# Decode steps emitted ahead of the first MLP, and the later attention's first q and k loaded amid the decode

## The chip, the cores and the metric

The kernel runs on one core of one Trainium2 chip. The metric is the device time of one launch in microseconds. Five engines work side by side, each through its own list of instructions in a fixed order: TensorE (matmuls and transposes, PE in the profile), VectorE (DVE), ScalarE (ACT), GpSimd (POOL) and SyncE (SP, which here mainly issues DMAs). An instruction that waits holds up all that stand behind it on its engine. The time before is 1550.24 us, the median of 3 runs (1548.09 to 1552.9).

## The reference

One layer of a hybrid decoder is computed for a prompt of 1024 tokens (width 1024) and for 32 sample tokens: 8 sequences of 4 tokens, each with 1024 earlier tokens whose K and V lie in a cache of 128-token pages, found through a page table.

```python
h = rms_norm(x, n1) * (1 + sc1) + sh1
proj = h @ w_in                       # 3 x 512 for attention, 4 x 512 for HGRN2
q_a, k_a = rms_norm(q_a, qg), rms_norm(k_a, kg)          # 8 heads x 64
z = einsum(q, k) * SB_SCALE + bias                       # stick-breaking attention
log_1m = where(valid, log_sigmoid(-z), 0)                # valid: key before query
w = where(valid, exp(log_sigmoid(z) + tail(log_1m)), 0)  # tail: sum over the later keys
o_a = einsum(w, v)
o_b = HGRN2(q, f, i, g, state)                           # gated recurrence, new state out
x = x + g1 * (concat(o_a, o_b) @ w_out)
h2 = rms_norm(x, n2) * (1 + sc2) + sh2
x = x + g2 * (square(relu(h2 @ w_up)) @ w_down)          # up to 4096, down to 1024
```

For the sample tokens K and V of the attention are the pages of the cache followed by the new tokens (the "decode"). Outputs are the two x, the new k and v, and the HGRN2 states.

## The kernel before

Weights and activations are split into a high and a low part, and each product is three matmuls (high x high, low x high, high x low; lines 204 to 206 and 1228 to 1230). The order of the work is: projections to about 200 us; HGRN2 and the attention of prompt tokens 0 to 511 to about 500; the output projection of these tokens, four token tiles of 128 (t = 0 to 3), to about 560; then a long stretch to about 1105 in which the first MLP (tokens 0 to 511) is interleaved with the decode and with the "later" attention (tokens 512 to 1023 against all 1024 keys); then the second output projection and the last MLP.

The output projection of a token tile ends in the residual `xr`, whose norm is worked out by ScalarE (`jk`, line 1167) and VectorE (lines 1169 to 1172); TensorE then transposes it (`ptx`, line 318), ScalarE scales it to `hf` (line 323) and VectorE splits it into `h_hi` and `h_lo` (lines 335, 336), the input of the MLP.

The first MLP goes through the hidden width in blocks of four pieces m = 0 to 3 of 128 columns. In its first block the up products are done for tokens 0 to 255 first (`pm`, 24 matmuls of 128x256 for each m), as these are ready before the tokens of tile 3, and then for tokens 256 to 511. The PSUM banks are given out by name: `M0 = "0123"` gives the four m of the first half the banks 0 to 3, `BM` gives later MLP tiles banks 0 and 1, and `BD = dict(z="4572", t="63", a="7")` gives the decode's transposes `ptd` banks 4, 5, 7 and 2 in turn, and its scores `pzd` banks 6 and 3. Whoever is emitted first gets a bank first.

The decode (line 563) builds its constants and the tile `qbd`, then walks through 64 K pages: a page is loaded by SP into `raw` (line 616, `NRAW = 4` buffers), transposed by TensorE (`ptd`, line 632, four transposes), copied to `kt` by ScalarE or VectorE (line 633), and after four pages their scores are added to `pzd` (line 638). `pzd` is copied to `dbe` (line 640) after 16 pages. Then two rounds `gz` (heads' halves of the batch) build `qbf` (line 645), the sigmoid weights `dbe` and `dom` (lines 653 to 660), and the V pages follow, interleaved with the decode of HGRN2. The attention (line 879) loads, for every head, `qh`, `ql` and `kk` from the scratch `qkd` and `vhl` from `vd`, all issued by POOL (lines 891 to 894, two buffers each), and computes scores `pz` (lines 905, 906).

Two generators, the MLP and `decode_and_attention`, are emitted in turn by `interleave`, with weights 64 and 166. A scheduler puts the instructions on each engine's list by their priority, which follows the order of emission, and by when it expects them to be ready; the lists are fixed when the program is built.

```python
interleave((mlp(*h2, [slice(0, 512)], rp, 2, ga), WM), (decode_and_attention(), W[3]))
```

Of the kernel before, what the change touches and what calls it, by code (L numbers as in the profile page):

```python
# [9 lines left out]
F32 = mybir.dt.float32  # L10
F32R = mybir.dt.float32r
# [9 lines left out]
P = 128  # L21
D = 1024
KT = 8
T = 1024
# [8 lines left out]
W = [66, 24, 9, 166, 4]  # L33
NBE0, NBE, NHB, NWA, NU, NRW, NX2, NF = 4,8,3,4,4,4,3,3
# [25 lines left out]
WM = 64  # L60
NPR = 2
NFX = 5
NSW = 5
NPL = 2
PQ0 = 100
AG = ()
BQ = "0167"
# [14 lines left out]
def hymba_step(ctx, tc, x_p, x_s, ck, cv, st_in, ptab, c_p, c_s, w_ada, b_ada, n1g, n2g, w_in,  # L82
# [3 lines left out]
    V, S, G, TE = nc.vector, nc.scalar, nc.gpsimd, nc.tensor  # L86
# [14 lines left out]
    def pool(name, side="left", stack=ctx, **kw):  # L101
        return stack.enter_context(tc.tile_pool(name=name, bufs=1, side=side, reuse_waits="tile", **kw))
# [7 lines left out]
    qkd = dp.tile([2, 2, 4, P, T], F32, name="qkd")  # L110
# [65 lines left out]
    def interleave(*steps, last=None):  # L176

        steps = [[g, n, 0] for g, n in steps]
        while steps:
            x = min(steps, key=lambda x: (x[2] + 0.5) / x[1])  # L180
            if next(x[0], x) is x:
                steps.remove(x)
                if x[0] is last:
                    return
            x[2] += 1
# [51 lines left out]
    def bank(kind, shape, name):  # L237
        turn[kind] = turn.get(kind, -1) + 1
        tag = banks[kind][turn[kind] % len(banks[kind])]
        return psum.tile(shape, F32, name=name, tag=f"bank{tag}", bufs=1)  # L240
# [262 lines left out]
    def qkv(px):  # L503
        for what, c0 in enumerate((QA, KA, VA)):
# [22 lines left out]
            for g in range(4):  # L527
                rows = slice(256 * g, 256 * (g + 1))
                x2 = pq.tile([P, 2, 512], F32, name="x2", bufs=NX2)
                for u in range(2):  # L530
# [7 lines left out]
                    yield  # L538
                with tc.high_priority(offset=PQ if what else PQ0):
                    if what < 2:  # L540
# [19 lines left out]
                                nc.sync.dma_start(qkd[what, part, 2 * p2:2 * p2 + 2, :, rows].rearrange("a p t -> p a t"),  # L560
                                                  tt.rearrange("p a u t -> p a (u t)").bitcast(F32))

    def decode(pd_):

        qbd = pd_.tile([P, 2, 544], F32, name="qbd", tag="qbd", bufs=1)
        G.memset(qbd, 0.0)
# [38 lines left out]
        ms = pd_.tile([P, 4, NB, 4], F32, name="ms")  # L605
# [35 lines left out]
        for gz in range(2):  # L641
            be = bes[gz]

            qbf = pd_.tile([P, 4, 32], F32, name="qbf")
            G.memset(qbf, 0.0)
            for p in range(4):
                for hh in range(2):
                    rr, o = slice(64 * hh, 64 * hh + 64), 4 * hh
                    S.copy(qbf[rr, p, :].rearrange("p (b x) -> p b x", x=8)[:, :, o:o + 4],
                           qTn[rr, p, 16 * gz:16 * gz + 16].rearrange("p (b t) -> p b t", t=4))  # L650
            pz = bank("t", [P, NS], "pzn")
            for p in range(4):
                TE.matmul(pz[32 * p:32 * p + 32], qbf[:, p, :], kTn[:, p, :], start=True, stop=True)
            V.tensor_tensor(be[:, T:], pz, tb[:, gz].rearrange("p b t -> p (b t)"), op=add)
            om = pd_.tile([P, NKEY + 1], F32, name="dom", tag="dom", bufs=1)
            G.memset(om[:, NKEY:NKEY + 1], 1.0)
            S.activation(om[:, 0:NKEY], be, AF.Sigmoid, bias=rbn, scale=-1.0)
            S.activation(be, be, AF.Sigmoid, bias=rbp)
            V.tensor_tensor_scan(om[:, 0:NKEY][:, ::-1], om[:, 0:NKEY][:, ::-1], om[:, 0:NKEY][:, ::-1], 1.0, op0=mult, op1=ALU.bypass)
            V.tensor_tensor(be, be, om[:, 1:NKEY + 1], op=mult)  # L660
            yield

            wt = pd_.tile([P, 9, 4, 32], F32, name="wt", tag="qbd", bufs=1)
            for k0 in (0, 4, 8):
                n, r = (4, P) if k0 < 8 else (1, NS)
                pt = bank("z", [P, 4, P], "ptdw")
                for u in range(n):
                    TE.transpose(pt[:r, u, :], be[:, (k0 + u) * P:(k0 + u) * P + r], ident)
                for u in range(n):
                    V.tensor_copy(wt[:r, k0 + u].rearrange("p b (q y) -> p b q y", y=8), pt[:r, u, :].rearrange("p (q b y) -> p b q y", q=4, y=8))  # L670
            yield

            pn = bank("z", [P, 512], "podn")
            TE.matmul(pn, wt[:NS, 8].rearrange("p b y -> p (b y)"), vn, start=True, stop=True)
            for b4 in range(4):
                b = 4 * gz + b4
                po = bank("a", [P, 512], "pod")
                for u in range(8):
                    if u % 4 == 0:
                        vt = pd_.tile([P, 4, 512], F32, name="vt", tag="kt", bufs=NKV)  # L680
                    load_page(vt[:, u % 4, :], cv, 8 * b + u)
                    g = slice(32 * (u % 4), 32 * (u % 4) + 32)
                    TE.matmul(po[g], wt[:, u, b4, :], vt[:, u % 4, :], start=(u < 4), stop=(u >= 4))
                    if u % 4 == 3:
                        yield
                od = pd_.tile([P, 512], F32, name="od", bufs=1)
                S.copy(od, po)
                g = slice(32 * b4, 32 * b4 + 32)
                V.tensor_tensor(od[g], od[g], pn[g], op=add)
                pt = bank("t", [P, 4 * P], "ptod")  # L690
                for p in range(4):
                    TE.transpose(pt[:, p * P:(p + 1) * P], od[:, p * P:(p + 1) * P], ident)
                ot = pd_.tile([P, 544], F32, name="ot", bufs=1)
                S.copy(ot[:, 0:512], pt)
                for hh in range(2):
                    r = slice(64 * hh, 64 * hh + 64)
                    src = ot[r].rearrange("p (q x) -> p q x", x=136)[:, :, 0:128].rearrange("p q (g x) -> p q x g", g=4)
                    V.tensor_reduce(ms[r, :, b, :], src[:, :, 4 * hh:4 * hh + 4, :], axis=AX.X, op=add)
                yield
# [176 lines left out]
        with tc.high_priority(offset=PH):  # L876
            norm()

    def attention(pb, ms, nbe):

        q0, nq, nk = 256 * ms[0], 256 * len(ms), 256 * (ms[-1] + 1)
        both = lambda t, part, p, r, cs: qkd[t, part, p, r, cs].unsqueeze(0).to_broadcast([2, 64, cs.stop - cs.start])
        for p in range(4):
            for hh in range(2):
                h = 2 * p + hh
                hr = slice(64 * hh, 64 * hh + 64)

                qh, ql = (pb.tile([P, nq], F32R, name=name, bufs=2) for name in ("qh", "ql"))
                kk_ = pb.tile([P, nk], F32R, name="kk", bufs=2)
                for part, tile_ in enumerate((qh, ql)):  # L890
                    G.dma_start(tile_, both(0, part, p, hr, slice(q0, q0 + nq)))
                G.dma_start(kk_, qkd[1, :, p, hr, 0:nk])
                vhl = pb.tile([P, nk // P, P], F32R, name="vhl", bufs=2)
                G.dma_start(vhl, vd[0:nk, P * h:P * (h + 1)].rearrange("(t p) x -> p t x", p=P))
                for m in ms:
                    ws = []
                    for i in (2 * m, 2 * m + 1):
                        n = (i + 1) * P
# [26 lines left out]
                    for kb in range(0, 2 * m + 2, 2):  # L925
# [12 lines left out]
                        for a in range(2):  # L938
                            cs = slice(P, 256) if diag and a == 1 else slice(0, 256)
# [22 lines left out]
    def hgrn_decode(p1):  # L962
# [63 lines left out]
        for j in range(4):  # L1026
# [8 lines left out]
    gq, ga = qkv(pool("qkv_w", stack=xstack)), pool("ada", side="right", stack=qstack)  # L1035
    ga = ada(AP0, lambda p=ga: p.tile([P, 512], F32, name="ar", tag="ar", bufs=2),
             lambda n, p=ga: p.tile([P, 2048], F32, name="wada", bufs=NAR)[:, 0:512 * n], "ada")
# [145 lines left out]
    def mlp(h_hi, h_lo, chunks, fp, nx, side=iter(())):  # L1183
# [1 line left out]
        r_hi = [h_hi[:, k] for k in range(KT)]  # L1185
        r_lo = [h_lo[:, k] for k in range(KT)]
        n = chunks[-1].stop
        g2b = fp.tile([P, D], F32, name="g2b")
        acc = [lp.tile([P, HW], F32, name=f"acc{c}", tag="acc", bufs=8) for c in range(KT)]
        for blk in range(NBLK):  # L1190
            u_hi, u_lo, ws = [], [], []
# [20 lines left out]
            if blk == 0:  # L1212
                for cs in parts:
                    for m in range(NK):
                        up(m, cs)
                    yield
            if blk == NBLK - 1:
                nc.sync.dma_start(g2b, g2d.to_broadcast([P, D]))
            for half_ in range(2):

# [29 lines left out]
    def last_mlp(h_hi, h_lo, fp):  # L1250
# [123 lines left out]
        for blk in range(NBLK):  # L1374
            u_hi, u_lo = ([lp.tile([P, HW], F32R, name=f"u{x}{m}", tag="u", bufs=8) for m in range(NK)] for x in "hl")
            if blk >= NPL:
                up([unit_weights(blk * FB_ + 2 * P * i) for i in range(2)], u_hi, u_lo)
# [61 lines left out]
    def decode_and_attention():  # L1439
        banks.update(BD)  # L1440
        with ExitStack() as es:
            gd = decode(pool("decode", stack=es))
            for _ in range(33):
                next(gd)
                yield
            banks.update(BV)
            yield from side_by_side((gd, 28), (hgrn_decode(pool("hgrn_s", stack=es)), W[4]))
        banks.update(BA)
        with ExitStack() as es:
            yield from attention(pool("attn1", stack=es), (2, 3), NBE)  # L1450

    def h2_tiles():
        return hp2.tile([P, KT, HW], F32R, name="h2_hi", tag="h2_hi", bufs=1), hp2.tile([P, KT, HW], F32R, name="h2_lo", tag="h2_lo", bufs=1)
# [3 lines left out]
    h2 = h2_tiles()  # L1457
# [7 lines left out]
    rp = pool("res", side="right", stack=rstack)  # L1465
# [1 line left out]
    banks.update(m0=M0)  # L1467
    gate = lambda: rp.tile([P, 512], F32, name="ar", tag="xres", bufs=2)
    ga = ada(AP1, gate, lambda n: wp.tile([P, 512 * n], F32, name="wada", tag="wraw", bufs=NWR), "m")
    interleave((mlp(*h2, [slice(0, 512)], rp, 2, ga), WM), (decode_and_attention(), W[3]))  # L1470
    h2 = h2_tiles()
    banks.update(o="45", r="36", s=BS)
    with ExitStack() as es:
# [37 lines left out]
```

## Time and profile before

| | |
|---|---|
| median of 3 runs | 1550.24 us (1548.09 to 1552.9) |
| profiled execution | 1546.85 us |
| its span in the trace | 1545.1 us |
| granted TensorE clock, mean | 0.988 of full speed |
| TensorE busy | 1489.3 us (96%), 9521 matmuls and transposes |
| VectorE busy | 1083.4 us (70%) |
| ScalarE busy | 642.7 us (42%) |
| POOL busy | 345.4 us (22%) |

A wait in the trace is the idle time of an engine just ahead of an instruction, with what released it ("<-"). The time of a matmul row is longer than the distance to the next one, since matmuls overlap in the array; what one costs is the distance between starts. The granted clock is the share of its full speed at which TensorE ran; 0.50 is the lower of its two levels, 1.2 instead of 2.4 GHz.

### The profile page before, as it was taken

Reading aid. Unit: us, or ns where it says so; the run is one execution under the profiler, and the core shown is the slowest. Engines: PE = TensorE matmul, PEld = TensorE weight load, DVE = VectorE, ACT = ScalarE, POOL = GpSimd, SP = SyncE. Lnnn points to the kernel's source line nnn. Section 1 sums busy time; section 2 is a strip of 40 time slices with the busy share of each in tenths; the row PEclk is TensorE's granted clock in tenths of the full one; section 3 lists DMA queues with packets and bytes.
Section 4 is the critical chain, followed back from the end, with each engine's and each line's share of the span. In section 5 each row is a group of like instructions: output and inputs, shape, how many; then the busy total and the mean of one; then the engine's idle time right before and its main releaser. Section 6 shows DMA issues by size and latency. Waiting matters only on the chain. (4 is left out here: it accounts for less than half of the span.)

```text
span 1545.1 us, 26232 instructions
## 1 busy us (share of the span) xinstructions
PE 1489.3 (96%) x9521; PEld 1257.0 (81%) x9521; DVE 1083.4 (70%) x2288; ACT 642.7 (42%) x1219; POOL 345.4 (22%) x560
## 2 busy tenths in 40 slices
PE   7999999999999989999997999999999999999998
PEld 3666689999999787775665788888578999999998
DVE  4976438888876783455554888888688567777775
ACT  3742234443422454333232666664245533343340
POOL 0200125634210030000121676694200000000000
PEclk8999999999999999999998999999999999999999
DMA  9389873423123456668677366552654333323222
GB/s 325 118 278 309 265 231 68 106 58 92 37 77 114 140 172 219 218 216 256 199 160 121 88 133 121 119 113 74 237 164 125 105 96 96 92 84 99 84 82 86
DMA packets 249414, 223.14 MB, mean 144 GB/s; under 512 B 60507, under 2 KB 196259, under 8 KB 247236
## 3 DMA queue, kind: packets, MB, share of 16 engines
q1 hardware_dynamic: 186308, 199.26, 41.0%
q0 software_dynamic: 62976, 22.20, 8.8%
q8 instruction: 75, 1.23, 0.3%
q14 instruction: 55, 0.45, 0.1%
HBM read 190.14 MB, written 31.11 MB: 143 GB/s over the span
## 5 line engine op out<-in xcount | busy, mean ns | idle before, releaser
L204 PE MATMUL pm<-h_hi,whi 128*128 128x384 f32 (+3 forms) x800 | 273.0, 343 | 6.0 <-DVE h_hi L335 3.0
L205 PE MATMUL pm<-h_lo,whi 128*128 128x384 f32 (+3 forms) x800 | 272.2, 341 | 0.3
L206 PE MATMUL pm<-h_hi,wlo 128*128 128x384 f32 (+3 forms) x800 | 271.7, 340 | 0.0
L151 ACT CAST whi<-wraw 128x1024 fp32r<-128x1024 f32 x136 | 142.8, 1053 | 217.8 <-PE pm L205 128.0
L152 DVE TENSOR_TENSOR wlo<-wraw,whi 128x1024 fp32r<-128x1024 f32 x128 | 169.1, 1321 | 89.6 <-ACT whi L151 83.6
L204 PEld LDWEIGHTS pm<-h_hi,whi 128*128 128x128 f32 x800 | 151.5, 190 | 24.3 <-issue 6.4
L206 PEld LDWEIGHTS pm<-h_hi,wlo 128*128 128x128 f32 x800 | 152.1, 190 | 10.6 <-issue 2.0
L205 PEld LDWEIGHTS pm<-h_lo,whi 128*128 128x128 f32 x800 | 152.2, 190 | 10.2 <-DVE h_lo L336 0.8
L206 PE MATMUL pm<-uh,wlo 128*128 128x272 f32 x512 | 145.2, 289 | 0.0
L205 PE MATMUL pm<-ul,whi 128*128 128x272 f32 x512 | 144.8, 288 | 0.0
L204 PE MATMUL pm<-uh,whi 128*128 128x272 f32 x512 | 139.8, 289 | 0.4 <-ACT uh L1327 0.4
L919 DVE TENSOR_TENSOR_SCAN om<-om 128x128 f32<-128x128 f32 (+3 forms) x96 | 112.3, 1174 | 25.4 <-POOL om L913 20.3
L1228 PE MATMUL pm<-whi,uh 128*128 128x512 f32 x256 | 104.7, 409 | 3.3 <-DVE acc L1236 3.3
L920 POOL TENSOR_TENSOR be<-be,om 128x384 f32<-128x384 f32 (+3 forms) x96 | 100.5, 1056 | 23.9 <-DVE om L919 20.0
L1229 PE MATMUL pm<-wlo,uh 128*128 128x512 f32 x256 | 101.9, 399 | 0.0
L1230 PE MATMUL pm<-whi,ul 128*128 128x512 f32 x256 | 101.7, 402 | 0.0
L205 PEld LDWEIGHTS pm<-ul,whi 128*128 128x128 f32 x512 | 95.9, 188 | 0.2 <-DVE ul L1328 0.2
L206 PEld LDWEIGHTS pm<-uh,wlo 128*128 128x128 f32 x512 | 95.9, 188 | 0.1
L204 PEld LDWEIGHTS pm<-uh,whi 128*128 128x128 f32 x512 | 93.4, 188 | 0.7 <-ACT uh L1327 0.7
L217 PE MATMUL pm_qkv<-whi,h_lo 128*128 128x512 f32 x192 | 77.3, 403 | 1.1 <-DVE h_lo L336 0.8
L215 PE MATMUL pm_qkv<-whi,h_hi 128*128 128x512 f32 x192 | 77.2, 403 | 0.4 <-DVE rs_i L138 0.3
L216 PE MATMUL pm_qkv<-wlo,h_hi 128*128 128x512 f32 x192 | 76.4, 398 | 0.0
(404 smaller groups left out, 3408.5 us busy)
## 6 DMA issues: line engine op xcount, KB each, us to landing
wraw<-in_w_down_dram SPq DMA_DIRECT2D x64, 512.0 KB, 5.7
wraw<-in_w_up_dram SPq DMA_DIRECT2D x40, 512.0 KB, 5.6
wada<-in_w_ada_dram SPq DMA_DIRECT2D x16, 1024.0 KB, 8.7
raw<-in_cache_k_dram SPq DMA_DIRECT2D x64, 256.0 KB, 3.2
vt<-in_cache_v_dram SPq DMA_DIRECT2D x64, 256.0 KB, 4.6
wraw<-in_w_in_dram SPq DMA_DIRECT2D x24, 512.0 KB, 5.9
uraw<-in_w_up_dram SPq DMA_DIRECT2D x24, 512.0 KB, 3.8
wa<-in_w_ada_dram SPq DMA_DIRECT2D x16, 512.0 KB, 6.4
```

What stands on the lines that cost most here:

```text
L151: (V.tensor_copy if h is V else S.copy)(hi, src)
L152: (e or V).tensor_tensor(lo, src, hi.bitcast(F32), op=sub)
L204: TE.matmul(pm, w_hi[:, k, :], r_hi[k][:, cs], start=(k == ks[0]), stop=False)
L205: TE.matmul(pm, w_hi[:, k, :], r_lo[k][:, cs], start=False, stop=False)
L206: TE.matmul(pm, w_lo[:, k, :], r_hi[k][:, cs], start=False, stop=(k == ks[-1]))
L215: TE.matmul(pm, h_hi[:, k, cs], hi, start=(k == 0), stop=False)
L217: TE.matmul(pm, h_lo[:, k, cs], hi, start=False, stop=(k == KT - 1))
L919: V.tensor_tensor_scan(back, back, back, 1.0 if right is None else right[:, 0:1], op0=mult, op1=ALU.bypass)
L920: G.tensor_tensor(be[:, 0:w], be[:, 0:w], om[:, 1:w + 1], op=mult)
L1228: TE.matmul(pm, u_hi[m][:, ts], hi, start=(m == 0), stop=False)
L1229: TE.matmul(pm, u_hi[m][:, ts], lo, start=False, stop=False)
L1230: TE.matmul(pm, u_lo[m][:, ts], hi, start=False, stop=(m == NK - 1))
```

## The change

Three edits belong together. First, `ND = 4` steps of `decode_and_attention` (the decode's set-up and its first six K pages) are emitted before `interleave` starts; with the first turn of `interleave`, which falls to the decode, eight pages are emitted before the first MLP tile. Second, q and k of head 0 of the later attention are loaded into three tiles of the residual pool (`qh0` and `ql0` in the two buffers with the tag `xres`, `kk0` in one with the tag `g2b`) by a function of its own, `load_qk`, marked to be issued after the MEMSET of `qbf` of the second half (`gz == 1`); the attention takes these tiles for head 0 and its own two buffers from head 1 on. Third, the MLP's tile `g2b` is allocated only in its last block, under the same tag, so that its load, and the loads of the residual tiles tagged `xres`, follow head 0's last use of the buffers.

```diff
+ND = 4
...
             qbf = pd_.tile([P, 4, 32], F32, name="qbf")
-            G.memset(qbf, 0.0)
+            mark = G.memset(qbf, 0.0)
+            if gz == 1:
+                with tc.issue_after(mark.ins):
+                    load_qk(*first, 0, 512, 512, T)
...
+    def load_qk(qh, ql, kk, h, q0, nq, nk):
+
+        hr = slice(64 * (h % 2), 64 * (h % 2) + 64)
+        for part, x in enumerate((qh, ql)):
+            G.dma_start(x, qkd[0, part, h // 2, hr, q0:q0 + nq].unsqueeze(0).to_broadcast([2, 64, nq]))
+        G.dma_start(kk, qkd[1, :, h // 2, hr, 0:nk])
+
+    def attention(pb, ms, nbe, first=None):
...
-                qh, ql = (pb.tile([P, nq], F32R, name=name, bufs=2) for name in ("qh", "ql"))
-                kk_ = pb.tile([P, nk], F32R, name="kk", bufs=2)
-                for part, tile_ in enumerate((qh, ql)):
-                    G.dma_start(tile_, both(0, part, p, hr, slice(q0, q0 + nq)))
-                G.dma_start(kk_, qkd[1, :, p, hr, 0:nk])
+                if h == 0 and first:
+                    qh, ql, kk_ = first
+                else:
+                    qh, ql = (pb.tile([P, nq], F32R, name=name, bufs=2) for name in ("qh", "ql"))
+                    kk_ = pb.tile([P, nk], F32R, name="kk", bufs=2)
+                    load_qk(qh, ql, kk_, h, q0, nq, nk)
...
-        g2b = fp.tile([P, D], F32, name="g2b")
...
             if blk == NBLK - 1:
+                g2b = fp.tile([P, D], F32, name="g2b", tag="g2b")
                 nc.sync.dma_start(g2b, g2d.to_broadcast([P, D]))
...
     def decode_and_attention():
         banks.update(BD)
         with ExitStack() as es:
-            gd = decode(pool("decode", stack=es))
+            first = [rp.tile([P, n], F32R, name=name, tag=tag, bufs=b)
+                     for name, n, tag, b in (("qh0", 512, "xres", 2), ("ql0", 512, "xres", 2), ("kk0", T, "g2b", 1))]
+            gd = decode(pool("decode", stack=es), first)
...
-            yield from attention(pool("attn1", stack=es), (2, 3), NBE)
+            yield from attention(pool("attn1", stack=es), (2, 3), NBE, first)
...
-    interleave((mlp(*h2, [slice(0, 512)], rp, 2, ga), WM), (decode_and_attention(), W[3]))
+    gda = decode_and_attention()
+    for _ in range(ND):
+        next(gda)
+    interleave((mlp(*h2, [slice(0, 512)], rp, 2, ga), WM), (gda, W[3]))
```

On TensorE, where the first MLP begins and the transposes `ptx` of token tile 3 (from `xr_6109` and `xr_6110`) stand, the list before reads as follows; `pm_6451`, `pm_6481` and `pm_6511` are the tiles m = 1, 2 and 3 of tokens 0 to 255, and `pm_6651` is m = 0 of tokens 256 to 511:

```order
L206 MATMUL pm_6451<-h2_hi_5763,wlo_6400 128x256
L205 MATMUL pm_6481<-h2_lo_5764,whi_6407 128x256
...
L206 MATMUL pm_6481<-h2_hi_5763,wlo_6408 128x256
L204 MATMUL pm_6511<-h2_hi_5763,whi_6415 128x256
...
L206 MATMUL pm_6511<-h2_hi_5763,wlo_6416 128x256
L318 MATMUL ptx_6303<-ident_73,xr_6109 128x128 x4
L318 MATMUL ptx_6315<-ident_73,xr_6110 128x128 x4
L204 MATMUL pm_6651<-h2_hi_5763,whi_6391 128x256
...
L632 MATMUL ptd_6555<-ident_73,raw_6544 128x128 x4
```

The tiles m = 2 and 3 stand ahead of the transposes. The same place after the change, up to the twentieth K page; `pm_6601`, `pm_6631` and `pm_6661` are m = 1, 2 and 3 of tokens 0 to 255 here, `pm_6799` is m = 0 of tokens 256 to 511, and `pzd_6384` holds the scores of the first 16 pages:

```order
L207 MATMUL pm_6601<-h2_hi_5763,wlo_6550 128x256
L319 MATMUL ptx_6303<-ident_73,xr_6109 128x128 x4
L319 MATMUL ptx_6315<-ident_73,xr_6110 128x128 x4
L205 MATMUL pm_6799<-h2_hi_5763,whi_6541 128x256
...
L634 MATMUL ptd_6487<-ident_73,raw_6476 128x128 x4
L640 MATMUL pzd_6384<-kt_6385,qbd_6338 32x512 x4
...
L205 MATMUL pm_6631<-h2_hi_5763,whi_6557 128x256
...
L634 MATMUL ptd_6703<-ident_73,raw_6692 128x128 x4
...
L634 MATMUL ptd_7062<-ident_73,raw_7051 128x128 x4
L205 MATMUL pm_6661<-h2_hi_5763,whi_6565 128x256
```

The 24 matmuls of m = 2 now stand behind the seventh page's transposes, the 24 of m = 3 behind the twentieth's, and the transposes `ptx` directly behind m = 1.

On POOL, around the MEMSET of `qbf` for the second half of the batch, the list before has the loads of head 0 of the later attention behind the last loads of the decode's HGRN2 states (`s0b`):

```order
L645 MEMSET qbf 128x128
L656 MEMSET dom 128x1
...
L972 DMA s0b_8405<-in_state_hgrn_dram 64x4x64 x2
L891 DMA qh<-qkd 128x1x512
L891 DMA ql<-qkd 128x1x512
L892 DMA kk<-qkd 128x1x1024
L894 DMA vhl<-vd 128x8x128
```

After the change the loads of q and k (`qh_6332`, `ql_6333`, `kk_6334`) stand behind that MEMSET:

```order
L647 MEMSET qbf 128x128
L888 DMA qh_6332<-qkd 128x1x512
L888 DMA ql_6333<-qkd 128x1x512
L889 DMA kk_6334<-qkd 128x1x1024
L661 MEMSET dom 128x1
...
L984 DMA s0b_8379<-in_state_hgrn_dram 64x4x64 x2
L906 DMA vhl<-vd 128x8x128
```

The three loads have moved ahead of the MEMSET of `dom` and of all the state loads; `vhl`, the values of head 0, has stayed.

## Rows read from the trace of the kernel before

**Rows 1.** The page: busy us and share of the span, TensorE's engine first.

```profile
PE 1489.3 (96%) x9521; PEld 1257.0 (81%) x9521; DVE 1083.4 (70%) x2288; ACT 642.7 (42%) x1219; POOL 345.4 (22%) x560
```

**Rows 2.** TensorE's waits: instruction, releaser, us in total, times, longest.

```profile
PE pz L905 <- DMA kk<-qkd: 11.7, 1, 11.7
PE ptx L318 <- DVE xr L1172: 3.8, 1, 3.8
```

**Rows 3.** Timeline of TensorE at 810: start, us, instruction, [idle before].

```profile
810.16 0.40 PE L1230 MATMUL pm<-whi,ul 128*128 128x512 f32 x1
...
822.22 0.45 PE L905 MATMUL pz<-kk,qh 128*128 128x128 f32 x1 [11.65 <-DMA kk<-qkd]
...
825.45 0.48 PE L1229 MATMUL pm<-wlo,uh 128*128 128x512 f32 x1
```

**Rows 4.** Windows of 2 us there: busy per engine, granted clock, DMA share, GB/s.

```profile
816.00:818.00 2.00, 0.00 (x0) 0.00 (x0) 0.00 (x0) 0.00 (x0) 0.00 (x0) 0.50 1.73 129
824.00:826.00 2.00, 2.00 (x7) 1.52 (x7) 1.71 (x3) 1.75 (x5) 1.32 (x2) 0.60 0.43 93
```

**Rows 5.** Timeline of POOL, two places.

```profile
664.27 0.20 POOL L645 MEMSET qbf<- 128x128 f32 x1 [46.37 <-PE pzn L653]
671.23 0.10 POOL L656 MEMSET dom<- 128x1 f32 x1 [6.75 <-DVE dbe L660]
...
798.48 0.83 POOL L892 DMA_DIRECT2D kk<-qkd  x1
```

**Rows 6.** Loads of `kk` between 700 and 900: issue to landing.

```profile
DMA to landing us min/median/max: 14.9/19.9/27.4
```

**Rows 7.** Windows, as rows 4, of two stretches.

```profile
660.00:670.00 10.00, 10.00 (x70) 7.75 (x69) 5.99 (x8) 5.52 (x13) 0.20 (x1) 1.00 0.71 205
850.00:900.00 50.00, 46.81 (x238) 38.44 (x237) 42.21 (x49) 31.60 (x58) 36.02 (x56) 1.00 0.41 98
```

**Rows 8.** POOL's use of `g2b`: count, shortest, median, longest ns, first and last start.

```profile
L1241 POOL TENSOR_TENSOR acc<-acc,g2b x8: 1285/1292/2280, 1015.2 to 1045.2; 128x512 f32<-128x512 f32 x8
```

**Rows 9.** Timeline of TensorE at 549 to 561.

```profile
549.15 0.28 PE L205 MATMUL pm<-h_lo,whi 128*128 128x256 f32 x1
...
554.62 0.28 PE L206 MATMUL pm<-h_hi,wlo 128*128 128x256 f32 x1
558.73 1.34 PE L318 MATMUL ptx<-ident,xr 128*128 128x128 f32 x8 [3.83 <-DVE xr L1172]
561.42 0.80 PE L204 MATMUL pm<-h_hi,whi 128*128 128x256 f32 x2 [1.34 <-DVE h_hi L335]
```

**Rows 10.** Timeline of VectorE before `xr`.

```profile
556.29 0.42 DVE L1199 TENSOR_TENSOR rr<-rr 128x256 f32<-128x256 f32 x1
...
557.18 0.42 DVE L1201 TENSOR_TENSOR ul<-rr,uh 128x256 fp32r<-128x256 f32 x1
...
558.10 0.88 DVE L1172 TENSOR_SCALAR xr<-xr,s 128x512 f32<-128x512 f32 x2
```

**Rows 11.** Timeline of ScalarE before `xr`.

```profile
548.88 0.63 ACT L1167 ACTIVATE jk<-xr 128x512 f32<-128x512 f32 x1 [2.89 <-DVE xr L1165]
...
549.50 2.89 ACT L323 ACTIVATE hf<-ptx,b,a 128x128 f32<-128x128 f32 x8
```

**Rows 12.** Timeline of TensorE at the first K pages.

```profile
569.24 0.60 PE L632 MATMUL ptd<-ident,raw 128*128 128x128 f32 x4
569.60 0.36 PE L204 MATMUL pm<-h_hi,whi 128*128 128x256 f32 x1
...
576.18 1.07 PE L638 MATMUL pzd<-kt,qbd 128*32 128x512 f32 x8
577.18 0.66 PE L632 MATMUL ptd<-ident,raw 128*128 128x128 f32 x4
```

**Rows 13.** Loads of K pages, 569 to 600: issues, then us to landing.

```profile
L616 SPq DMA_DIRECT2D raw<-in_cache_k_dram x18: 332/333/1382, 569.9 to 599.1; - x18
...
DMA to landing us min/median/max: 2.8/3.4/8.0
```

**Rows 14.** TensorE's waits between 562 and 810.

```profile
PE pm L204 <- DVE h_hi L335: 1.3, 1, 1.3
```

**Rows 15.** Window, as rows 4, at the K pages.

```profile
576.00:578.00 2.00, 2.00 (x18) 1.02 (x17) 1.22 (x5) 1.61 (x4) 0.00 (x0) 1.00 1.10 362
```

More of the change, by code (lines that the diff above doesn't have):

```diff
@@ L561, in qkv, with decode @@
                                                   tt.rearrange("p a u t -> p a (u t)").bitcast(F32))
-    def decode(pd_):
+    def decode(pd_, first):
         qbd = pd_.tile([P, 2, 544], F32, name="qbd", tag="qbd", bufs=1)
@@ L877, in hgrn @@
             norm()
-    def attention(pb, ms, nbe):
+    def load_qk(qh, ql, kk, h, q0, nq, nk):
[4 more added lines that the diff above has]
+    def attention(pb, ms, nbe, first=None):
         q0, nq, nk = 256 * ms[0], 256 * len(ms), 256 * (ms[-1] + 1)
-        both = lambda t, part, p, r, cs: qkd[t, part, p, r, cs].unsqueeze(0).to_broadcast([2, 64, cs.stop - cs.start])
         for p in range(4):
```

## The prediction

> **What bounds the kernel now.** I read the page first: TensorE is busy 1489.3 of 1545.1 us [rows 1], so nearly all of the time is matmuls, which the change neither adds nor removes, and what can move is the 55.8 us in which TensorE sits idle, plus the slow clock behind long idles. The list of TensorE's waits [rows 2] shows that idle time in small pieces; one of them, 11.65 us for `kk`, stands out, and the second, 3.83 us for `xr`, lies exactly where the change alters the order. The reader should see in the timeline of TensorE [rows 3] that the last matmul of the MLP before the hole starts at 810.16 and the first scores of the later attention at 822.22, and in the 2 us windows [rows 4] that the granted clock falls to 0.50 during the hole. The timeline shows the first matmul shorter than 0.6 us at 825.45: 3.2 us of work ran at the lower of the two levels (1.2 instead of 2.4 GHz). POOL explains the hole [rows 5]: it issues `kk` of head 0 only at 798.48, behind the last state loads, and such loads land after 14.9 to 27.4 us [rows 6].
>
> **Part one, the early load of head 0.** The three loads now stand behind the MEMSET of `qbf` for the second half of the heads, which POOL ran at 664.27 [rows 5]. Even with the slowest landing of 27.4 us they are there before 700, while the scores stood at 822; they move forward in TensorE's order, over the MLP matmuls ahead of them, but by no 100 us. So the wait of 11.65 us goes, and with it the low clock that followed: work that took 3.2 us takes 1.6. Gain 11.65 + 1.6 = 13.3 us. What is late next: the values `vhl` of head 0, which POOL still issues at the old place, right behind the old `kk`; but the first product with them keeps its place in TensorE's order, far behind the scores, so I add nothing. From about the middle of this attention on the order of TensorE is the same in both, so nothing else is bought or paid there. Head 1 and head 2 now take the two ordinary buffers at once; their loads are issued where those of heads 0 and 1 were, a head earlier than before.
>
> The three issues on POOL take about 2.5 us (0.83 for one [rows 5]) ahead of a MEMSET that waited 6.75 us for VectorE [rows 5]: hidden, 0; without that cover 2.5 us. They bring 1 MB forward, about 5 us at the 205 GB/s that the queues carried at 660 to 670 [rows 7]. TensorE is at 10.00 of 10 us there, and the queues are at 0.71: I take 0, between 0 and 5 us of loss. The Trainium skill, "DMA: Bandwidth & Descriptors", section "Issuing engines are not separate DMA queues", says that transfers issued by different engines run on the same 16 engines and interleave, so that POOL's megabyte delays the pages and weights which SyncE asks for. By the row the net stands as below; by the rule alone it would be up to 5 us worse.
>
> The loads of `xres` and `g2b` on SP move behind head 0's last scores, since they share these buffers. SP then issues them during the attention instead of beside the first K pages; they are read in the MLP's last block, by POOL from 1015.2 us on [rows 8], some 190 us after the scores: 0, and a landing of a few us only if that block stood right behind them, which it does not.
>
> **Part two, four decode steps ahead of the MLP.** The matmuls are the same; their order at the seam between output projection and MLP is not, and every engine runs its instructions in order. The MLP's tiles m = 2 and 3 of the first 256 tokens use banks 2 and 3. Emitted first, they got them first. Now eight page transposes, one of them in bank 2, and the scores `pzd` of the decode, in bank 3 until 16 pages are through, hold them first. Two things follow.
>
> First, 47 matmuls of 128x256, which start at 549.15 and end at about 554.8 [rows 9], leave the place ahead of `ptx`, the transposes of token tile 3. One is 0.119 us (554.62 - 549.15 over 46 steps): 5.6 to 5.7 us of work gone from in front of a wait. `ptx` started at 558.73 after 3.83 us of idle time, released by VectorE's `xr` at 558.10 [rows 9, 10]. Two VectorE operations of the moved tiles, at 556.29 and 557.18, stood inside that chain, about 0.35 us of issue each, partly in gaps (I count 0.3 for both), and ScalarE may do two `hf` of 0.36 us (2.89/8) before instead of after an idle of 2.89 us [rows 11]. So `xr` comes some 1.0 us sooner, `ptx` at 557.7. TensorE is dry from 549.2: 8.5 us of idle instead of 3.83, loss 4.7. Bounds: 3.7 if `xr` comes 2 us sooner, 5.7 if not at all. The next wait, 1.34 us for `h_hi` [rows 9], stays.
>
> Second, the 20 K pages behind it stand almost without MLP work in between: pages 1 to 4 with about 10 matmuls, pages 5 to 8 with the 24 of m = 2, pages 9 to 20 with none. Four page buffers are there. The row of the loads says that a buffer is asked for again about 0.6 us after its transposes start (569.24, load issued 569.9), and the load lands in 3.4 us (2.8 to 8.0) [rows 12, 13]: a cycle of 4.0 us for four pages. The transposes of a page take 0.36 us of TensorE (569.24 to 569.60) and a scores group of four 0.5 (576.18 to 577.18 for eight) [rows 12]: 1.95 for four pages. From the first page: TensorE is through with page 4 at 2.5, page 5 is there at 4.0: idle 1.5. Pages 5 to 8 with the 24 matmuls (2.9 us) end at 8.8, no wait. Page 13 can come at 12.8, TensorE is ready at 10.75: idle 2.1. Page 17 the same, 2.1. Loss 5.6 (rounded), after which m = 3 takes over and TensorE has work again. Bounds: 0 if the pages never hold TensorE; with every landing at 8.0, three waits grow by 4.6 each and the second round waits 3.9: 5.6 + 13.8 + 3.9 = 23.3.
>
> Between 562 and 810 us TensorE waited for nothing but 1.3 us for `h_hi` [rows 14], for no bank and no page, so by the rows of before alone part two would cost nothing. The Trainium skill, "Perfetto Trace Analysis", section "Optimization Strategy", says that regular bubbles can mean that there is not enough SBUF or PSUM for the next tile to be allocated; that speaks against this change. By the rows alone the net would be -13.3, with the rule it is the sum that follows.
>
> **The sum.** -13.3 + 4.7 + 5.6 = -3.0 us. The profiled execution took 1546.85 us (1545.1 of span and 1.75 around it), so 1543.85 for its twin; the median of the runs is 1550.24, 3.4 above it, so I forecast 1550.24 - 3.0 = 1547.2 us. A measurement of this kernel can tell about 0.3%, 4.65 us, from no change; so the likeliest case is just inside "no difference". Its own range, from the bounds of the hole (1.0 either way) and landings of 2.8 to 4.5 us (three waits, -1.8 to +3.3): -6 to +1.5, 1544 to 1552.
>
> **The rivals.**
> A first one: the pages do not hold TensorE. For it: before, TensorE waited nowhere on a page [rows 14], and the 256 KB are small. Against it: then always MLP work stood between. Gain 13.3 - 4.7 = 8.6, 1541.6 us.
> The slow one: page landing decides. Each of the waits for a page grows with the landing time, and pages 5 to 20 share the queues with the MLP's weights, which at 576 to 578 already carried 362 GB/s at a share of 1.10 [rows 15]. At 8.0 us, the slowest of the 18 loads, the loss is 4.7 + 23.3 = 28.0, the net +14.7, 1565 us. It is slower than before from a landing of 3.4 + 3.0/3 = 4.4 us, measurably from about 6.0 (4.65 more, over three waits). Against it: the median is 3.4, over the 18 loads of the window at the seam.
> Another: the early load does not do what it says, because the scores of head 0, now earlier, wait for their bank or find the loads behind decode traffic, or VectorE and POOL give the gain back in the attention. POOL is at 36 and VectorE at 42 of 50 us there [rows 7]; against it, TensorE is idle only 3.2 us in those 50. The whole gain lost: +10.3, 1560.5 us; half of it, +3.7.
>
> **How the numbers follow.** The main case 0.52: 0.16 of it faster by over 0.3%, 0.34 within, 0.02 slower. Pages without a hold 0.22, all faster. Page landing slow 0.14, all counted as slower. Early load without effect or given back 0.12: 0.08 slower, 0.04 within. Together faster 0.38, same 0.38, slower 0.24. The range from 1538 to 1558 leaves out the far half of the slow case, the upper part of the last case and a little on the fast side, where hole and pages cost less than their bounds: about 2 in 10.
>
> **What would show it.** The wait `pz <- kk` is missing from the list of waits, the granted clock stays at 1.00 from 780 to 830, and the first `pz` of the later attention starts within 25 us of 790. `ptx` of tile 3 waits 8 to 9 us for `xr` where it waited 3.83. Page transposes `ptd` of the first 20 pages wait for `raw` by the DMA, 5 to 6 us in three or four pieces; none of it would prove the first rival, over 10 us the slow one. If the wait for `kk` is gone but its 13 us appear at a later attention wait on VectorE or POOL, the third is right. I would be wrong altogether if the hole at 549 us stayed as it was, because something else fills TensorE there, or if the low clock spread over the stretch of the pages.

## The result, and the profile after

The changed kernel takes 1569.07 us, median of 4 runs (1565.71 to 1572.0), against 1550.42 us before: ratio 1.0119, 95% interval 1.0094 to 1.0145, 18.7 us slower. 1547.2 was forecast, with 1558 as the upper end. The profiled execution has a span of 1564.0 us. All ratios here compare the fast runs alone; one run of the kernel before and one of a changed kernel, both near 3690 us, are left out of them.

The page after: the busy time of the engines, as in [rows 1].

```profile
PE 1498.1 (96%) x9521; PEld 1259.8 (81%) x9521; DVE 1080.7 (69%) x2288; ACT 642.0 (41%) x1219; POOL 346.4 (22%) x560
```

The same 9521 matmuls keep TensorE busy 8.8 us longer, so only about half of the loss is idle time. The list of TensorE's waits, which answers to [rows 2]:

```profile
PE ptd L634 <- DMA raw<-in_cache_k_dram: 11.4, 6, 6.5
PE ptx L319 <- DVE xr L1184: 8.3, 1, 8.3
```

The wait for `kk` is gone, as forecast. `ptx` waits 8.3 us for `xr`, and the page transposes wait 11.4 us for K pages, 6.5 of it at one place. TensorE's timeline has `ptx`, then the five waits for the first 20 pages, then the long one and the first scores of the later attention (start, us, instruction, [idle before]):

```profile
559.73 1.94 PE L319 MATMUL ptx<-ident,xr 128*128 128x128 f32 x8 [8.30 <-DVE xr L1184]
...
573.22 0.63 PE L634 MATMUL ptd<-ident,raw 128*128 128x128 f32 x4 [0.93 <-DMA raw<-in_cache_k_dram]
574.32 0.63 PE L634 MATMUL ptd<-ident,raw 128*128 128x128 f32 x4 [0.47 <-DMA raw<-in_cache_k_dram]
...
583.91 0.63 PE L634 MATMUL ptd<-ident,raw 128*128 128x128 f32 x4 [0.85 <-DMA raw<-in_cache_k_dram]
...
587.38 0.63 PE L634 MATMUL ptd<-ident,raw 128*128 128x128 f32 x4 [1.85 <-DMA raw<-in_cache_k_dram]
...
593.15 0.63 PE L634 MATMUL ptd<-ident,raw 128*128 128x128 f32 x4 [0.84 <-DMA raw<-in_cache_k_dram]
...
690.07 1.08 PE L634 MATMUL ptd<-ident,raw 128*128 128x128 f32 x4 [6.50 <-DMA raw<-in_cache_k_dram]
...
815.05 0.39 PE L917 MATMUL pz<-kk,qh 128*128 128x512 f32 x1
```

What the long wait is for: POOL's timeline at that place, which answers to [rows 5], SP's page loads there, and the landing of the two pages loaded between 676 and 691 (against [rows 13]).

```profile
676.45 0.20 POOL L647 MEMSET qbf<- 128x128 f32 x1 [40.08 <-PE pzn L658]
676.60 0.85 POOL L888 DMA_DIRECT2D qh<-qkd  x1
677.45 0.81 POOL L888 DMA_DIRECT2D ql<-qkd  x1
678.23 0.82 POOL L889 DMA_DIRECT2D kk<-qkd  x1
```

```profile
678.65 0.92 SPq L618 DMA_DIRECT2D raw<-in_cache_k_dram  x2
```

```profile
DMA to landing us min/median/max: 11.7/11.7/11.7
```

POOL issues the megabyte from 676.6 to 679.1; its three loads land after 10.9, 17.2 and 24.6 us, and the two pages that SP asks for from 678.65 on after 11.7 us, where the median was 3.4. The windows, as in [rows 4], show the granted clock behind that hole:

```profile
684.00:690.00 6.00, 0.00 (x0) 0.00 (x0) 0.91 (x2) 0.00 (x0) 0.00 (x0) 0.65 1.15 248
690.00:696.00 6.00, 5.93 (x18) 4.85 (x19) 0.69 (x1) 0.59 (x1) 0.00 (x0) 0.50 0.80 204
```

From the transposes of token tile 2 to the first matmul of the second output projection the kernel before took 554.5 us (544.95 to 1099.46), the changed one 571.1 (547.06 to 1118.16): 16.6 of the 18.9 us between the spans. Of the other 2.3 us, 2.1 lie ahead of the stretch, whose start scatters from 544.95 to 549.17 among the traces of this case. Idle time in this stretch rose by 6.2 us: +4.5 at `ptx`, +4.9 at the first 20 pages, +6.5 at the long page wait, -11.65 at `kk`, +1.9 in small waits, the longest behind the first scores. The other 10.4 us are work that takes longer. Adding up the distances from start to start (idle left out), the decode's value products `pod` (line 683 before, 688 after) take 24.9 us instead of 19.8, its transposes `ptd` 29.2 instead of 26.0, 0.9 of it at the low clock; what is left is 2.1. That is what the low clock adds elsewhere: in the stretch TensorE works at it for 14.8 us instead of 8.8, half of the difference is 3.0, and `ptd` has 0.9 of that.

### The profile page after: what moved, and what is told of

It reads as the page before. It is cut to its first block, busy times and chain, and to the rows that moved or that the text cites. A ratio compares the mean times of both kernels' runs of the same rounds, so it can differ in the third digit from the quotient of the medians.

```text
span 1564.0 us, 26240 instructions
## 1 busy us (share of the span) xinstructions
PE 1498.1 (96%) x9521; PEld 1259.8 (81%) x9521; DVE 1080.7 (69%) x2288; ACT 642.0 (41%) x1219; POOL 346.4 (22%) x560
## 5 line engine op out<-in xcount | busy, mean ns | idle before, releaser
L153 DVE TENSOR_TENSOR wlo<-wraw,whi 128x1024 fp32r<-128x1024 f32 x128 | 165.1, 1290 | 83.3 <-ACT whi L152 82.0
L206 PEld LDWEIGHTS pm<-h_lo,whi 128*128 128x128 f32 x800 | 151.7, 190 | 11.3 <-issue 2.1
L932 POOL TENSOR_TENSOR be<-be,om 128x384 f32<-128x384 f32 (+3 forms) x96 | 103.8, 1090 | 24.6 <-DVE om L931 18.9
```

The lines of the kernel that those rows point to most:

```text
L153: (e or V).tensor_tensor(lo, src, hi.bitcast(F32), op=sub)
L206: TE.matmul(pm, w_hi[:, k, :], r_lo[k][:, cs], start=False, stop=False)
L932: G.tensor_tensor(be[:, 0:w], be[:, 0:w], om[:, 1:w + 1], op=mult)
```

## The experiments

Two theories at first: A, the loss is the sum of the seam, the first pages, the early load that meets the last K pages, and `pod`; B, the load is harmless and all comes from the moved decode.

**The load alone.** `ND = 4` becomes `ND = 0`; TensorE's order at the seam and that of `pod` are those of before.

> Only the early load is kept (ND = 0: no decode step ahead of the MLP); TensorE's order at the seam and the value products of the decode are those of before. Theory A (the early load meets the last K pages on the queues): the wait for kk goes, -13.3 us against before, and K pages that are under way behind POOL's loads land in over 8 us; TensorE waits for a page 0 to 6.5 us and runs slow behind it, so -13 to -4 us. Theory B (the load is harmless, the long page wait of the changed kernel comes from the moved decode): -13.3 us, no page lands later than 8 us and TensorE waits for none.

1547.52 us, ratio 0.9982 (0.9964 to 0.9999). Its profiled execution, the fastest of its twelve runs, waits for pages three times:

```profile
PE ptd L634 <- DMA raw<-in_cache_k_dram: 4.6, 3, 2.4
```

Pages wait, so B's first half falls; but only some 3 of the 13.3 us are gained, less than A said.

**The decode steps alone**, in the kernel before:

```diff
+ND = 4
...
-    interleave((mlp(*h2, [slice(0, 512)], rp, 2, ga), WM), (decode_and_attention(), W[3]))
+    gda = decode_and_attention()
+    for _ in range(ND):
+        next(gda)
+    interleave((mlp(*h2, [slice(0, 512)], rp, 2, ga), WM), (gda, W[3]))
```

> Only the four decode steps ahead of the MLP, with the loads of before. Theory A: the hole ahead of the token-tile transposes (+4.5), the first 20 K pages (+4.5 to 7) and value products that are split from groups of four into smaller runs (26 runs' worth instead of 21, about 1 us each, +5) all stay, the wait for kk stays too: +14 to +17 us against before, no page wait above 3 us near 680. Theory B: the page wait of 6.5 us and its slow clock stay as well: +23 to +26.

1566.92 us, ratio 1.0099 (1.0078 to 1.0120): by the ratio +15.4, within A's +14 to +17. A single run of the same kernel gives its trace.

> The four decode steps ahead of the MLP alone, for its trace. Theory A as before: ptx waits 8.3 us, the first 20 pages 4 to 5, no page wait near 680, kk still waits 11 us. If kk no longer waits, the moved decode itself pays for that wait, and an early load can gain nothing beside it.

TensorE's waits there, and ScalarE's between 800 and 840:

```profile
PE pm L1229 <- ACT rr L1199: 8.5, 1, 8.5
PE ptx L319 <- DVE xr L1173: 8.3, 1, 8.3
PE ptd L633 <- DMA raw<-in_cache_k_dram: 5.5, 5, 3.0
```

```profile
ACT whi L152 <- DMA wraw<-in_w_up_dram: 12.7, 1, 12.7
```

No long page wait, but `kk` doesn't wait either, against A. By their times POOL's loads, issued from 808.8 on, now hold up a weight piece (`wraw`) that SP issued at 810.5: ScalarE waits for it 12.7 us and TensorE 8.5, and half of the 4.1 us of work at the low clock behind it makes 10.5. The attention's first loads cost about the same wherever they run into something: 13.3 us at `kk` before, 10.5 at the weight piece here, 9.4 at the last K pages in the changed kernel (6.5 idle and 2.9 of low clock).

**The load later**, amid the V pages, with and without the decode steps:

```diff
+LQ = (0, 2)
...
                 S.copy(od, po)
+                if (gz, b4) == LQ:
+                    lq = pd_.tile([1, 1], F32, name="lq")
+                    mark = G.tensor_copy(lq, od[0:1, 0:1])
+                    with tc.issue_after(mark.ins):
+                        load_qk(*first, 0, 512, 512, T)
```

> The whole change, but POOL issues the early load amid the V pages (behind the third group of values, after all K pages) instead of amid the last K pages; TensorE's order is the same as in the changed kernel, instruction for instruction. Theory A: the 6.5 us page wait and the slow stretch behind it (2.9) go, kk does not wait: 9 us faster than the changed kernel, +9 us against before. Theory B: the same as the changed kernel, +18.7.

1567.0 us, 1.0119 (1.0093 to 1.0145). The long page wait is gone, and the time is that of the changed kernel: by the number B, by the trace neither, since `s0b` (2.3 us), `ptdw` (2.1) and a granted clock of 0.90 from 750 to 800 stand in its place.

> Only the early load, issued amid the V pages; no decode step ahead of the MLP; TensorE's order is the same as with the early load alone. Theory A: -13.3 us against before, and faster than the load amid the K pages by what TensorE waits for pages there. Theory B: -13.3, the same as the load amid the K pages. If V pages are as sensitive as K pages, a wait of TensorE on vt appears and half of the gain is lost.

1550.99 us, 1.0004 (0.9986 to 1.0021). Nothing is gained:

```profile
PE pos L1002 <- DMA s0b<-in_state_hgrn_dram: 7.5, 1, 7.5
```

**The load by SP**, amid the V pages (issued at 721 to 723, POOL's alone at 726 to 728), and behind the last V page. The edit of the first, against the changed kernel with `ND = 0`:

```diff
-                with tc.issue_after(mark.ins):
-                    load_qk(*first, 0, 512, 512, T)
+                with tc.issue_after(page_dmas[-1]):
+                    load_qk(*(x.bitcast(F32) for x in first), 0, 512, 512, T, nc.sync)
...
-        G.dma_start(kk, qkd[1, :, h // 2, hr, 0:nk])
+        eng.dma_start(kk, qkd[1, :, h // 2, hr, 0:nk])
```

> The early load alone (ND = 0), issued by SP amid the V pages instead of by POOL; TensorE's order is the same as with POOL's early load. Theory C (POOL's loads are the trouble: moved amid the K pages they delayed pages, amid the V pages they delayed the state loads s0b, each time by about what the wait for kk had cost): SP's loads land in under 10 us, nothing waits in their place, -10 to -13 us against before. Theory D (any early megabyte costs as much as it saves): -3 to +1, with a wait on s0b, vt or raw of 4 us or more.

1546.4 us, 0.9977 (0.9964 to 0.9990): a third of what C said. ScalarE waits 7.8 us for a weight piece that SP issued at 732.7, behind the burst; VectorE's `acc` stands behind the split of this piece, and TensorE waits 3.95 us for `acc` at 753. The queues were not full meanwhile (window as [rows 4]):

```profile
742.00:745.00 3.00, 3.00 (x14) 2.44 (x13) 2.97 (x3) 0.60 (x1) 0.00 (x0) 1.00 0.13 52
```

They moved 52 GB/s at a share of 0.13, where with POOL's burst they moved 248 at 1.15 (684 to 690 above). How SP's burst holds up a piece behind it is not settled.

> The early load alone (ND = 0), issued by SP right behind the last V page (about 784 us) instead of amid the V pages; TensorE's order as with the other early loads. Theory C2 (the megabyte costs only as long as pages or state loads share the queues with it): kk does not wait, nothing waits in its place, -10 to -13 us against before and 6 to 9 faster than amid the pages. Theory D2 (the load still takes over 20 us, so that scores wait again): -3 to 0, with a wait on kk of some us.

1550.71 us, 1.0001 (0.9989 to 1.0012), by D2. Issued this late, it is late again:

```profile
PE pz L918 <- DMA kk<-qkd: 5.4, 1, 5.4
```

> The whole change (ND = 4), with the load by SP behind the last V page; TensorE's order is that of the changed kernel. If the decode steps alone cost +15.4 and the load is now harmless: 15.4 - 10 to 13 = +2 to +5 against before. If the decode steps' own delay had already hidden the wait for kk, so that the early load has nothing left to gain: +14 to +17.

1578.01 us, 1.0176 (1.0160 to 1.0193), worse than either expectation: TensorE waits 12.7 us for `ve` on VectorE. Why VectorE was that late was not followed up.

**The value products.** In groups of four, each on its own quarter of the array's columns, they stand in TensorE's fixed order partly together and partly with other matmuls in between, most of them the MLP's. Count a unit for up to four that stand together: 21 before, 26 in the changed kernel. (A `pos`, itself on 32 columns, does not part them: at 703.77 in the kernel before two products and the four `pos` between them take 0.88 us.) The eighth group is whole before and parted by `patts` after (each product is recorded twice, so x8 is four):

```profile
728.76 1.07 PE L683 MATMUL pod<-vt,wt 128*32 128x512 f32 x8
```

```profile
747.84 1.05 PE L688 MATMUL pod<-vt,wt 128*32 128x512 f32 x2
748.81 0.25 PE L995 MATMUL patts<-smp_q,smp_k 64*32 64x32 f32 x2
748.99 1.06 PE L688 MATMUL pod<-vt,wt 128*32 128x512 f32 x6
```

The probe measures a unit by itself, with work behind the kernel's end that is used for nothing.

> The kernel before with a probe behind its end that adds to the output nothing: 16 products of 128x32 by 128x512 like pod, one for each quarter of the array's columns in turn, and 16 of 128x128 by 128x512 like the MLP's, in runs of four and four, two and two, one and one. Theory P: a run of four, of two and of one all take about 1.0 us, so 16 products take 4, 8 and 16 us beside the 16 MLP products (3.7 us). Theory Q: the run length does not matter, 4 us in all three.

Its timeline, runs of four, two and one (columns as above):

```profile
1612.85 1.06 PE L1497 MATMUL probe_q<-pa,pw 128*32 128x512 f32 x8
1613.85 1.19 PE L1500 MATMUL probe_m<-pr,prw 128*128 128x512 f32 x4
1614.97 1.06 PE L1497 MATMUL probe_q<-pa,pw 128*32 128x512 f32 x8
...
1620.57 1.05 PE L1497 MATMUL probe_q<-pa,pw 128*32 128x512 f32 x4
1621.55 0.73 PE L1500 MATMUL probe_m<-pr,prw 128*128 128x512 f32 x2
...
1645.15 1.05 PE L1497 MATMUL probe_q<-pa,pw 128*32 128x512 f32 x2
1646.12 0.49 PE L1500 MATMUL probe_m<-pr,prw 128*128 128x512 f32 x1
1646.55 1.05 PE L1497 MATMUL probe_q<-pa,pw 128*32 128x512 f32 x2
```

From start to start 1.00, 0.98 and 0.97 us for four, two and one: P is right, and sixteen take 4, 8 or 16 us. The five further units of the changed kernel are the 5.1 us of its `pod`. The MLP's products pay too: four and four take 2.12 us together, four times one and one 5.60, so a parting costs 1.16 us in all.

Keeping the fours together by a critical section failed twice:

> The kernel before with one edit: the four value products of a group (pod, one for each quarter of the array's columns) are kept together in TensorE's order. Theory P (four of them side by side take the 1.0 us of one, so each broken group costs another 1.0): 16 units instead of 21, -5 us against before. Theory Q (the split has no price, or waiting for the last of four pages eats it): 0, within 2 us.

1568.58 us, 1.0114 (1.0093 to 1.0136): the fours stand later in the order, and the waits outweigh the units (`pod` for `vt` 8.3 us, `ptos` for VectorE 7.0). Of P this shows only that each of the 16 units takes 1.1 us, or 1.9 at the low clock.

> The early load by SP and the value products kept in fours, no decode step ahead of the MLP. Theories C and P together: -13 and -5, -15 to -18 us against before, 1533 us. With Q: -10 to -13; with D: -5 to -8.

1595.34 us, 1.0295 (1.0275 to 1.0315), with `pod` waiting 15.3 us for SP's load.

**The seam put back.** The MLP's first step is emitted ahead of the four decode steps:

```diff
+    gda, gm = decode_and_attention(), mlp(*h2, [slice(0, 512)], rp, 2, ga)
+    next(gm)
+    for _ in range(ND):
+        next(gda)
+    interleave((gm, WM), (gda, W[3]))
```

> The four decode steps ahead of the MLP, but behind the MLP's first step, so that the tiles m = 2 and 3 stand ahead of the token-tile transposes as before; loads as before, the wait for kk stays. The hole at 549 us and the waits for the first 20 pages should go. The value products fall into 34 units here instead of 21. Theory P: +13 us against before. Theory Q: 0, within 3 us.

1576.45 us, 1.0168 (1.0148 to 1.0189). `ptx` waits 3.8 us again and no page waits: the seam's part is confirmed. `pod` takes 33.0 us instead of 19.8, 13.1 more for 13 units, as P says. The rest, some 13 us although `kk` does not wait, is new waits (8.8 for `acc`, 4.0 for `be`) and the low clock behind them.

Then with the page that comes last asked for first, which lets the other three stand behind it:

```diff
-                    TE.matmul(po[g], wt[:, u, b4, :], vt[:, u % 4, :], start=(u < 4), stop=(u >= 4))
+                    if u % 4 == 3:
+                        for i in (3, 2, 1, 0):
+                            v = u - 3 + i
+                            TE.matmul(po[32 * i:32 * i + 32], wt[:, v, b4, :], vt[:, i, :], start=(v < 4), stop=(v >= 4))
```

> The four decode steps ahead of the MLP, but behind its first step, with the value products last page first: 20 units instead of 34. Loads as before. Theory P: 13 to 14 us less than the same kernel without the edit, +12 against before; what is left over is no seam and no split. Theory Q: +26 as without.

1544.8 us, 0.9964 (0.9950 to 0.9978): 32 us better than without the edit, of which `pod` (19.6 us) makes 13.4; the rest came with the new order, and neither theory expected it (+12 and +26 against before). In this order four decode steps ahead are no loss.

> The changed kernel with one edit: in each group of four value products the one whose page comes last is asked for first, so that the other three stand directly behind it: 20 units in TensorE's order instead of 26 (before: 21). Theory P (a unit is 1.0 us however many of the four it holds): -6 us against the changed kernel, +12.5 against before. Theory Q (the waits elsewhere absorb it): as the changed kernel, +18.7.

1579.43 us, 1.0189 (1.0168 to 1.0210). `pod` falls to 19.3 us, by 5.7 for six units as P says, and yet the kernel is 10 us slower than the changed one: the whole order behind the first `pod` differs, TensorE's idle time in the whole kernel is 10.2 us higher, 4.1 of it a wait of the second output projection for `woraw`. So the price of a unit is shown, but not that this kernel would gain it.

**The load in pieces**, behind the groups of V pages, by SP, `ND = 0`:

```diff
+LQ0 = 4
...
+                        piece_ = 2 * (b4 + 4 * gz) + u // 4 - LQ0
+                        if 0 <= piece_ < 8:
...
+                            with tc.issue_after(page_dmas[-1]):
+                                if piece_ < 4:
...
+                                    nc.sync.dma_start(x[:, cs], qkd[0, piece_ // 2, 0, 0:64, 512 + cs.start:512 + cs.stop].unsqueeze(0).to_broadcast([2, 64, 256]))
+                                else:
+                                    cs = slice(256 * (piece_ - 4), 256 * (piece_ - 3))
+                                    nc.sync.dma_start(kk0[:, cs], qkd[1, :, 0, 0:64, cs])
```

These are two halves of `qh`, two of `ql` and four quarters of `kk`.

> The early load alone (ND = 0), by SP, cut into eight pieces of 128 KB, each behind one group of four V pages, from the fifth group on (some 50 us). Theory B (it is the megabyte in one burst that holds up whatever else is under way): kk does not wait, no page, state or weight waits over 2 us, -9 to -12 us against before. Theory E (the bytes cost their time however they are spread): -3 to 0, as in one burst.

1539.92 us, 0.9941 (0.9926 to 0.9956), -10.8 by the medians and -9.1 by the ratio, by theory B. SP issues the pieces from 703.5 to 759, and the first scores start without a wait:

```profile
802.39 0.22 PE L925 MATMUL pz<-kk,qh 128*128 128x128 f32 x1
```

Page, state and `kk` waits are gone. It is the burst, not the bytes; but size, pace and row length of the pieces changed together (a row of `kk` is 1 KB instead of 4), and which of them counts was not parted. With the last page first as well:

> The load in eight pieces and the value products last page first (20 units instead of 22 in the kernel with the pieces alone). Theories B and P: -11 to -14 us against before, 1537 us, the fastest here. With E and P: -5 to -1.

1539.36 us, 0.9939 (0.9920 to 0.9958), -11.3 by the medians and -9.5 by the ratio. The intervals do not part it from the run without (units 20 against 22); both are faster than both kernels of this case.

## Why the prediction was wrong, point by point

- **The hole ahead of `ptx`**: right. 8.30 us against 8.5 forecast; it went back to 3.8 when the MLP's first step came first.
- **The first 20 pages**: right in kind and size. 4.9 us of waits in five places against 5.6; with them the transposes themselves take longer, part of the +3.2 of `ptd`.
- **"TensorE is at 10.00 of 10 us there ... I take 0, between 0 and 5 us of loss"**, the price of the megabyte: failed, and not only in size. Full occupation of TensorE in [rows 7] showed that pages came in time without the load, not that there was slack. The burst was not through in 5 us either; its `kk` landed after 24.6. It more than tripled the landing of a page, 3.4 to 11.7 us: 6.5 us idle, and the low clock until 695.8 adds half of 5.7 us, 2.9. Together 9.4 of the 13.3 us gained. With the same order on TensorE and the load amid the V pages this wait is gone. The Trainium skill, "DMA: Bandwidth & Descriptors", section "Issuing engines are not separate DMA queues", says that transfers run on the same 16 engines whichever engine issues them. The trace agrees: SP's pages waited behind POOL's load, and SP's own burst gained no more within the intervals (-3.3 against -2.9 us).
- **"nearly all of the time is matmuls, which the change neither adds nor removes, and what can move is the 55.8 us in which TensorE sits idle"**: failed. The matmuls are the same, their time is not: 10.4 of the 16.6 us in the stretch are work. The orders were compared at the seam and for the attention ("the order of TensorE is the same in both, so nothing else is bought or paid there"), and the V stage has no term in the sum. There the four decode steps shift which products stand together: 5 more units, +5.1 us. The Trainium skill, "TensorEngine Tiling (Array Packing)", section "Key Properties", says that different tiles of the array can execute in parallel; the probe agrees, 1.00 us for four and 0.97 for one.
- **The gain of 13.3 us** counted as if it stood beside the rest: failed. With the decode steps alone `kk` no longer waits, since the load holds up a weight piece instead. The load brings -2.9 us alone. On top of the decode steps it brings nothing that these runs show: +18.7 us with it, +15.4 without, from two comparisons of their own whose intervals overlap. So the loss is that of the decode steps, and the load only moved a wait.
- **The slow rival** (page landing decides) named the mechanism, but that its 1565 us lie near is luck: it placed the wait at the seam and blamed the MLP's weights; the longest page wait was at the other end of the decode, and POOL's load made it.

By terms: 4.5 + 4.9 + 9.4 + 5.1 - 13.3 = 10.6 of the 16.6 us in the stretch. What is left, about 6, is 2.3 in the transposes outside the low clock, 1.9 in small waits and 1.7 of low clock from 839.4 to 842.8, behind three of these waits (1.57, 0.57, 0.63 us from 835 to 838; another of 2.12 is at 889). The first of them is also there with the load amid the V pages (1.6), so the place of the load did not bring it; for the others that is not settled.

## What to carry to other kernels

A load that is moved earlier is priced by what is under way where it lands: look for the transfer with the smallest margin there, and cut the load to the size and pace of its neighbours; in one burst it gained 0 to 3 us here, in eight pieces 9 to 11. When a change moves code in an order that a scheduler makes, count in the new lists of the engine, to the end of the stage, the groups that run side by side in the array, before saying that the work is the same. A wait removed and a delay added upstream of it are not two terms of one sum.

## What was not expected of the hardware

A product on 32 of the array's columns takes 0.97 us, and four on four quarters, standing together, take 1.00; one matmul of another shape between them (an MLP product on the whole array, or `patts` on 64 rows) costs the whole advantage.
